# A hybrid decoder layer: weight sums on VectorE across the mLSTM, the last branch's weights stored split, and the branch projections' PSUM halves swapped

## The chip, the core and the metric

The kernel runs on one core of a Trainium2 chip. A core has a matrix engine (TensorE, PE in the profile), three engines for elementwise work (VectorE or DVE, ScalarE or ACT, GpSimd or POOL) and a queue engine (SyncE, SP) that issues most DMAs. Each engine works through its own instructions strictly in order and waits on semaphores for the others. The metric is the device time of one execution in microseconds (us).

## The reference

One layer of a decoder over 1024 positions of width 1024, in float32. After a normalisation, three branches run side by side on `h`: a chunkwise mLSTM, a differential attention, and a cross-attention into 256 memory tokens. Each branch's output is projected, multiplied by a sigmoid gate and summed; `w_out` and an MLP follow.

```python
h = rms_norm(x, norm_mix_g[l])
proj = h @ w_in[l]
...
y_m = jax.nn.sigmoid(mo) * rms_norm(hm, m_norm_g[l]...)          # mLSTM, chunks of 128 positions
y_d = diff_attention(dq, dk, dv, ...)
y_c = memory_cross_attention(cq, mem, ...)
g_m, g_d, g_c = jnp.split(jax.nn.sigmoid(h @ w_gate[l] + b_gate[l]), N_BRANCH, axis=-1)
merged = g_m * (y_m @ w_proj_m[l]) + g_d * (y_d @ w_proj_d[l]) + g_c * (y_c @ w_proj_c[l])
x = x + merged @ w_out[l]
h2 = rms_norm(x, norm_mlp_g[l])
x = x + jnp.square(jax.nn.relu(h2 @ w_up[l])) @ w_down[l]
```

## The kernel before

**Number format.** A matrix operand is kept as a pair: `hi`, the value rounded to the matrix engine's fast 32-bit format (`F32R`), and `lo`, what the rounding lost. A product is three matmuls: hi·hi, hi·lo, lo·hi. Making a pair is a *split*: ScalarE casts, VectorE subtracts (`split2`, `split`; their lines are L114 and L121 on ScalarE, L69 and L123 on VectorE).

**Stages.** Transposes and the memory branch (0 to about 196 us), the mLSTM (to 640), the differential attention (to 1150), the gates (`wino_gates`, to 1240), the three branch projections (`branches`, to 1478), `w_out` in four groups (to 1573), the MLP's up half (to about 1890) and its down half (to the end).

**The mLSTM.** TensorE's order is written out by hand: `weave(stream(), items)` walks along a stream of projection matmuls `mm<-hT,w` and calls the function of an item when its position in the stream comes. `add(p, f)` puts `f` at position `p`; the stream has about 520 positions. The items are the gate chain (`m_gates`, `m_gates2`: the tiles `g_two`, `g_m`, `g_c`, `g_col`), and eight half heads of four chunks. A chunk needs a mask tile `ngb`, a weight tile `wib` (both loaded from DRAM, where the gate chain stored them as `g_dng` and `g_dwi`), the running state `C` with its split `Ch`, and the output `hS` with its norm `hss`. Instructions outside TensorE's written order are placed by a scheduler, per engine.

**Branch projections.** Each of the three products of 1024x1024x1024 is computed by Winograd's scheme: 7 products of quadrants in place of 8, which needs sums of the quadrants of the weights `wq` and of the rows `y`. 84 steps: three branches in the order (2, 0, 1), seven passes each, four steps a pass, 12 matmuls of 128x512 a step. A step n also splits its weights (`w<-raw`) and its rows (`xs<-row`) five steps ahead. The result of a pass is in four PSUM banks; `evict` takes them through `te` tiles (or directly) to VectorE, which multiplies by the gates (`gl`, fetched from `gates`), adds the branches so far (`mg`) and splits the sum into `mh` and `ml`, the operands of `w_out`.

**The early sums.** For the sums that need only inputs, or results of the memory branch, `early_sums` runs ahead, during the mLSTM: 16 groups of four loads of 256 KB (tiles `es`, in the pool of the next stage's weights), four GpSimd additions or subtractions of 128x512 (L1443 to L1446, L1449 to L1452) and four stores (L1456) into DRAM (`ws`, `xc`). `branches` reads them back. They are added to the items at positions 20 to 486, but only TensorE's order is tied to these; the scheduler has put them between about 185 and 365 us.

**Banks and what follows.** The branch passes take PSUM banks in two halves (`mm0` to `mm3`, `mm4` to `mm7`) by turns; the four groups of `w_out` do too, and the MLP's first products follow in banks from `p0` on. The MLP's weights are Winograd sums too: `wino_steps` loads `wraw`, GpSimd makes four sums (L1292 to L1295) and ScalarE and VectorE split them into `wo`. The MLP's input norm needs `ssq`, a sum of squares that GpSimd builds during `w_out` (L1722), which TensorE adds up in `px<-ones,ssq`.

Of the kernel before, what the change touches and what calls it, by code (L numbers as in the profile page):

```python
# [10 lines left out]
F32 = mybir.dt.float32  # L11
F32R = mybir.dt.float32r
# [5 lines left out]
P = 128  # L18
D = 1024
S = 1024  # L20
# [11 lines left out]
def f32(ap):  # L32
    return ap.bitcast(F32)
# [40 lines left out]
class Layer:  # L74
# [11 lines left out]
    nmm, kmm = 0, 2  # L86
    turned, stored, relus = [], {}, {}
    marks = {}

    def pin(self, ins):  # L90
        if self.pinned:
            self.tc.keep_in_program_order(ins)

    def mm(self, out, l, r, start, stop):
        self.pin(self.nc.tensor.matmul(out, l, r, start=start, stop=stop))  # L95

    def transpose(self, out, x):
        self.pin(self.nc.tensor.transpose(out, x, self.ident))
# [360 lines left out]
    gnext = None  # L459
# [137 lines left out]
    def branch_m(self, pool, gp, tail, gnext):  # L597
        nc, a = self.nc, self.a
        V, G = nc.vector, nc.gpsimd
        W = 32  # L600
# [234 lines left out]
        one = lambda: next(piece, None)  # L835
# [35 lines left out]
        for n in range(8):  # L871
            hd, hf = heads[n // 2], n % 2
            e = Epos[n]
# [423 lines left out]
    def wino_steps(self, srcs, wrp, wop, lead):  # L1297


        raws, W = [], []  # L1300

        def raw():
            n = len(raws)
            if n < len(srcs):
                r = wrp.tile([P, 8, P], F32, tag="wraw", name=self.name("wraw"))
                self.nc.sync.dma_start(r[:, 0:4], srcs[n])
# [12 lines left out]
        return raw, wsp, W  # L1319
# [104 lines left out]
    PASS = ((0, 0), (1, 2), (4, 4), (3, 3), (5, 5), (6, 1), (2, 6))  # L1424
    WOUT = (0, 2, 4, 6, 1, 3, 5, 7)

    def early_sums(self, pool):

        G, a = self.nc.gpsimd, self.a
        dt = lambda n: self.nc.dram_tensor(n, (4, 4, P, 512), F32).ap()  # L1430
        self.ws = [dt(f"ws{b}") for b in range(3)]
        self.xc = dt("xc_d")

        def chunk(srcs, dst, rows):
            new = lambda: pool.tile([P, 2, 256], F32, tag="w", name=self.name("es")).rearrange("p a b -> p (a b)")
            t = [new() for _ in range(4)]
            for o, s in zip(t, srcs):
                self.nc.sync.dma_start(o, s)
            yield
            e = new()  # L1440
            b0, b1, b2, b3 = t
            if rows:
                G.tensor_sub(e, b2, b0)  # L1443
                G.tensor_sub(b0, b0, b1)
                G.tensor_sub(b2, b2, b0)
                G.tensor_sub(b3, b3, b2)  # L1446
                outs = (b0, b2, e, b3)
            else:
                G.tensor_sub(e, b1, b0)  # L1449
                G.tensor_add(b3, b3, b0)  # L1450
                G.tensor_sub(b0, b3, b1)
                G.tensor_sub(b2, b2, b0)  # L1452
                outs = (b3, b0, e, b2)
            yield
            for i, o in enumerate(outs):
                self.nc.sync.dma_start(dst[i], o)  # L1456
            yield

        for b in (2, 0, 1):
            for kp in range(4):  # L1460
                yield from chunk([a["wq"][b, i, kp] for i in range(4)], self.ws[b][:, kp], False)
        for kp in range(4):
            yield from chunk([self.y_quad(2, i, kp) for i in range(4)], self.xc[:, kp], True)

    def y_quad(self, b, i, kp):
        k, hf = divmod(i, 2)
# [2 lines left out]
    def branches(self, pools, fetch, hi, lo):  # L1469
# [13 lines left out]
        def load(n):  # L1483
            if n >= N + 4:
                return
            wr[n] = t = self.rp.tile([P, 512], F32, tag="raw", name=self.name("raw"))
# [12 lines left out]

        def split(n, f):  # L1500
            if n >= N + 4:
                return
            w = self.wp.tile([P, 2, 512], F32R, tag="w", name=self.name("w"))
            f(w[:, 0], w[:, 1], wr.pop(n))
            if n >= N:
                w0.extend((w[:, 0, i * 256 : i * 256 + 256], w[:, 1, i * 256 : i * 256 + 256]) for i in range(2))
# [3 lines left out]
            W[n], X[n] = w, x  # L1510
# [33 lines left out]
        def out(bi, u, m, hf, c, late):  # L1544
            ft = 2 * u + m
            t = gates.pop(0)
            if bi == 0:
                o = mg[ft, hf] = mlp.tile([P, 512], F32, tag="ml", name=self.name("mg"))
                V.scalar_tensor_tensor(out=o, in0=t, scalar=1.0, in1=c, op0=ALU.add, op1=ALU.mult)
            elif bi == 1:  # L1550
                V.scalar_tensor_tensor(out=t, in0=t, scalar=1.0, in1=c, op0=ALU.add, op1=ALU.mult)
                G.tensor_add(mg[ft, hf], mg[ft, hf], t)
            else:
                V.scalar_tensor_tensor(out=t, in0=t, scalar=1.0, in1=c, op0=ALU.add, op1=ALU.mult)
                (V if late else G).tensor_add(t, mg[ft, hf], t)

                def keep():
                    lo[ft, hf] = mlp.tile([P, 512], F32R, tag="ml", name=self.name("ml"))
                    hi[ft, hf] = mtp.tile([P, 512], F32R, tag="mh", name=self.name("mh"))
                    self.split2(hi[ft, hf], lo[ft, hf], t)  # L1560
                    gate()

                return keep
            gate()

        def evict(bi, p, u, ps):
            new = lambda i: te[i].tile([P, 512], F32, tag="te", name=self.name("te"))
            if p in (0, 3):
                T[u] = new(u)
                A.copy(T[u], ps)  # L1570
            elif p == 2:
                S[u] = new(4 + u)
                A.copy(S[u], ps)
            elif p in (1, 4):
                V.tensor_add(T[u], T[u], ps)
                return out(bi, u, *((0, 1) if p == 1 else (1, 0)), T[u], False)
            elif p == 5:
                V.tensor_add(S[u], S[u], ps)
                return out(bi, u, 0, 0, S[u], False)
            else:  # L1580
                return out(bi, u, 1, 1, ps, True)

# [80 lines left out]
    def tail(self):  # L1663
# [11 lines left out]
        with ExitStack() as c0:  # L1675
# [9 lines left out]
            with ExitStack() as c1:  # L1685
                E = lambda *x, **k: c1.enter_context(tc.tile_pool(*x, **k))
                self.pmm, self.kmm, self.nmm = Banks(E, "pmm2"), 8, 3
                if True:
# [5 lines left out]
                    te = [one(f"te{i}") for i in range(3)]  # L1694
                    hole = E(name="hole", bufs=1).tile([P, 256], F32, name="hole")
                    xd = E(name="xd", bufs=20)
                    te += [one(f"te{i}") for i in range(3, 8)]
# [478 lines left out]
```

## Time and profile before

| what | us |
|---|---|
| runs, median of 3 (lowest, highest) | 2207.85 (2203.75, 2211.08) |
| the profiled execution | 2204.02 |
| its span in the profile | 2202.2 |
| TensorE busy | 2126.5 |
| VectorE busy | 1560.5 |
| ScalarE busy | 1051.1 |
| GpSimd busy | 735.5 |

A line of the profile gives the source line and engine, the operation, its output and inputs by the program's names, and shapes. In a timeline the two first numbers are start and duration in us, and the brackets give the idle time of that engine just before, and what ended it. Matmuls of one kind in a row are one line, with their count behind an x. TensorE's clock is reported as the share of full speed that was granted. Many operations pass through helpers, so one line number (L69, L95, L114, L121, L123) stands for many places, and the tile names tell them apart.

### The profile page before, as it was taken

What the parts mean: (1) busy time and instruction counts of PE and PEld (TensorE: products, weight loads), DVE (VectorE), ACT (ScalarE), POOL (GpSimd) and SP (SyncE); (2) the same over time, 40 slices, a digit from 0 to 9 for tenths busy, and PEclk for the clock granted to TensorE, in tenths of its full rate; (3) what the DMA queues carried; (4) which work ended last, traced back from release to release, by engine and by line L of the source; (5) the groups of instructions that cost most, each with busy time, mean ns of one, the idle gap of its engine ahead of it and who ended that gap; (6) DMA issues with size and microseconds to landing.
All of it is one profiled execution on the core that took longest, in us unless ns stands there. A gap on an engine that the chain in (4) does not pass through costs nothing. (4 is left out here: it accounts for less than half of the span.)

```text
span 2202.2 us, 31307 instructions
## 1 busy us (share of the span) xinstructions
PE 2126.5 (97%) x10905; PEld 1836.4 (83%) x10905; DVE 1560.5 (71%) x2841; ACT 1051.1 (48%) x2155; POOL 735.5 (33%) x844
## 2 busy tenths in 40 slices
PE   7999798999999999999999999989899999999999
PEld 5888577898899999999887887778788888888887
DVE  6644565665557877777656588985378888876698
ACT  6643233544435666666545545354344544543331
POOL 2102553000011111111013044532445677665563
PEclk9999898999999999999999999999999999999999
DMA  6127675222144333333334784446524544844443
GB/s 241 40 72 247 233 243 182 68 64 71 42 169 104 97 96 87 88 93 87 106 126 133 260 299 141 137 135 221 174 84 156 208 157 157 298 158 155 158 158 106
DMA packets 167973, 322.16 MB, mean 146 GB/s; under 512 B 16737, under 2 KB 33414, under 8 KB 165766
## 3 DMA queue, kind: packets, MB, share of 16 engines
q1 hardware_dynamic: 161478, 300.22, 42.6%
q10 hardware_dynamic: 6336, 19.93, 2.3%
q8 instruction: 86, 1.41, 0.3%
q14 instruction: 73, 0.60, 0.1%
HBM read 206.81 MB, written 88.11 MB: 134 GB/s over the span
## 5 line engine op out<-in xcount | busy, mean ns | idle before, releaser
L95 PE MATMUL mm<-w,hT 128*128 128x384 f32 (+3 forms) x2496 | 473.4, 333 | 5.3 <-DVE gf L645 3.9
L95 PE MATMUL mm<-hT,w 128*128 128x512 f32 x1680 | 414.5, 398 | 0.9 <-ACT gt L500 0.9
L95 PEld LDWEIGHTS mm<-w,hT 128*128 128x128 f32 x2496 | 392.6, 191 | 16.3 <-issue 2.3
L95 PEld LDWEIGHTS mm<-hT,w 128*128 128x128 f32 x1680 | 313.1, 191 | 62.8 <-ACT gt L500 1.3
L95 PE MATMUL p<-xo,wo 128*128 128x512 f32 x1344 | 309.7, 392 | 6.5 <-DVE gl L1715 6.2
L95 PE MATMUL p<-xd,wo 128*128 128x512 f32 x1344 | 305.4, 389 | 0.4 <-DVE u L69 0.4
L95 PEld LDWEIGHTS p<-xo,wo 128*128 128x128 f32 x1344 | 253.7, 189 | 61.1 <-DVE gl L1715 7.3
L95 PEld LDWEIGHTS p<-xd,wo 128*128 128x128 f32 x1344 | 252.0, 188 | 53.6 <-DVE u L69 1.1
L1609 PE MATMUL mm<-xs,w 128*128 128x512 f32 x1008 | 232.4, 392 | 5.8 <-DVE xs L69 4.9
L1609 PEld LDWEIGHTS mm<-xs,w 128*128 128x128 f32 x1008 | 189.9, 189 | 48.2 <-DVE xs L69 7.4
L114 ACT CAST wo<-wraw 128x896 fp32r<-128x896 f32 x124 | 116.9, 945 | 225.8 <-PE p L95 85.4
L69 DVE TENSOR_TENSOR wo<-wraw,wo 128x896 fp32r<-128x896 f32 x124 | 151.1, 1228 | 47.2 <-ACT wo L114 47.1
L1292 POOL TENSOR_TENSOR wraw<-wraw 128x128 f32<-128x128 f32 x128 | 97.1, 758 | 220.4 <-DMA wraw<-in_wdown 109.1
L123 DVE TENSOR_TENSOR w<-raw,w 128x256 fp32r<-128x256 f32 (+4 forms) x257 | 141.3, 575 | 34.5 <-ACT w L121 33.9
L1041 ACT ACTIVATE dpe<-sc,dst,drr 128x256 f32<-128x256 f32 (+7 forms) x128 | 106.6, 833 | 97.2 <-DVE dst L1037 96.7
L121 ACT CAST w<-raw 128x256 fp32r<-128x256 f32 (+4 forms) x257 | 116.1, 487 | 49.8 <-PE mm L95 14.6
L148 POOL TENSOR_SCALAR drr<-drr 128x16 f32<-128x16 f32 x16 | 3.3, 204 | 311.0 <-DVE drr L988 311.0
L1033 DVE CUSTOM_DVE_ANT_0 sc<-sc,tmask 128x256 f32<-128x256 f32 (+7 forms) x128 | 97.0, 758 | 13.6 <-PE sc L95 12.8
L114 ACT CAST w<-raw 128x512 fp32r<-128x512 f32 x83 | 51.7, 624 | 90.2 <-DMA raw<-ws 45.6
L1294 POOL TENSOR_TENSOR wraw<-wraw 128x128 f32<-128x128 f32 x128 | 93.1, 727 | 0.0
L95 PE MATMUL sc<-dk,dq 128*128 128x512 f32 (+3 forms) x384 | 91.9, 347 | 0.0
L69 DVE TENSOR_TENSOR acc<-acc,p 128x512 f32<-128x512 f32 x121 | 79.9, 683 | 14.9 <-PE p L95 13.9
(338 smaller groups left out, 3524.5 us busy)
## 6 DMA issues: line engine op xcount, KB each, us to landing
dk<-dsg SPq DMA_DIRECT2D x64, 256.0 KB, 4.2
wraw<-in_wup SPq DMA_DIRECT2D x64, 256.0 KB, 3.1
r_d<-xts SPq DMA_DIRECT2D x16, 1024.0 KB, 4.7
wraw<-in_wdown SPq DMA_DIRECT2D x64, 256.0 KB, 3.1
es<-in_wq SPq DMA_DIRECT2D x48, 256.0 KB, 3.8
ws<-es SPq DMA_DIRECT2D x48, 256.0 KB, 2.0
raw<-in_wd SPq DMA_DIRECT2D x32, 384.0 KB, 3.3
raw<-ws SPq DMA_DIRECT2D x48, 256.0 KB, 3.4
```

The lines of the kernel that those rows point to most:

```text
L69: return self.tc.keep_in_program_order(f(*a, **k))
L95: self.pin(self.nc.tensor.matmul(out, l, r, start=start, stop=stop))
L114: self.cast = self.A.copy(hi, src).ins
L121: a = nc.scalar.copy(hi, src)
L123: return a, nc.vector.tensor_sub(lo, src, f32(hi))
L148: g.tensor_scalar(r, ss, 1.0 / width, EPS, op0=ALU.mult, op1=ALU.add)
L1033: V.tensor_tensor_reduce(out=sc[:, 0:n], in0=sc[:, 0:n], in1=self.tmask[:, D - n : D], scale=1.0, scalar=-3.0e38, op0=ALU.add, op1=ALU.max ...
L1041: nc.scalar.activation(pe[c][:, 0:n], sc[:, 0:n], AF.Exp, bias=t8[:, 2 + c : 3 + c], scale=rr[:, i, c : c + 1], accum_out=t8[:, 4 + c : 5 ...
L1292: G.tensor_add(r[:, 4], r[:, 0], r[:, 3])
L1294: G.tensor_sub(r[:, 6], r[:, 1], r[:, 0])
L1609: nc.tensor.matmul(cur[u], w[:, l, c], x[:, m], start=first and i == 0, stop=last and i == 2, skip_group_check=True)
```

## The change

1. `early_sums` becomes `early`. The 12 groups of sums for the branches 2 and 0 and the rows `xc` run on VectorE instead of GpSimd. For branch 1, the last, eight half groups (`pairs`) compute all seven weight combinations on VectorE and ScalarE, split them, and store the pairs hi|lo in DRAM (`wh`). Each step is tied to a stream position on every engine: `behind(ins, self.mark)` lets the scheduler place it only behind the matmul that stood last when the step was called. Loads stand at p, sums at p + 8, stores from p + 12. The groups start at 2, 19, 36 and then from 112 on, the last at 504.
2. In steps 56 to 83 (the last branch) `branches` loads the pair straight into the ring of split weights: no cast and no subtraction. Its addition at the sixth pass (p == 5) goes from GpSimd to VectorE.
3. The branch passes use the other half of the banks, with the four banks of a pass rotated by two; `nmm = 3` shifts the groups of `w_out` likewise, so that the last ends on the low half.
4. The first load of an MLP weight after this is tied behind the last branch matmul (`hold`). The `te` tiles stand in another order in memory.

```diff
-        early = self.early_sums(gnext)
-        for i in range(16):
-            for at in (20, 28, 36):
-                add(at + 30 * i, next, early)
+        self.early(gnext, add)
...
+    def early(self, pool, add):
...
+        self.wh = dt("wh", (7, 4, P, 2, 512))
...
+        def at(p, f):
+            def g():
+                for i in f():
+                    self.behind(i.ins, self.mark)
+
+            add(p, g)
...
+            return [(V.tensor_sub if o == "sub" else V.tensor_add)(*q) for o, *q in ops]
...
+            def cut(i):
+                q = t[i]
+                return [A.copy(q[:, 0], v(q)), V.tensor_sub(q[:, 1], v(q), f32(q[:, 0]))]
...
+            at(p, load)
+            at(p + 8, calc)
+            for i in range(7):
+                at(p + 10 + i, lambda i=i: cut(i))
+                at(p + 13 + i, lambda i=i: keep(i))
...
+        p = 2
+        for _ in range(3):
+            sums(p, *S.pop(0))
+            p += 17
+        p = 112
+        for n in range(8):
+            pairs(p, 1, n // 2, n % 2)
+            p += 29
+            sums(p, *S.pop(0))
+            p += 20
+        sums(p, *S.pop(0))
...
+            if 56 <= n < N:
+                bi, p, kp = where(n)
+                l, x = self.PASS[p]
+                W[n] = w = self.wp.tile([P, 2, 512], F32R, tag="w", name=self.name("w"))
+                nc.sync.dma_start(f32(w), self.wh[l, kp])
...
             elif p == 5:
                 V.tensor_add(S[u], S[u], ps)
-                return out(bi, u, 0, 0, S[u], False)
+                return out(bi, u, 0, 0, S[u], True)
...
-                        self.pmm.tile([P, 512], F32, tag=f"mm{4 - g % 2 * 4 + u}", name=self.name("mm")) for u in range(4)
+                        self.pmm.tile([P, 512], F32, tag=f"mm{g % 2 * 4 + (u + 2) % 4}", name=self.name("mm")) for u in range(4)
...
         self.pinned = False
+        self.hold = self.mark
...
-                    self.nmm = 7
+                    self.nmm = 3
```

SyncE's order where the gate chain's results go to DRAM and come back as the first `ngb` and `wib`, before:

```order
L1438 DMA es_3514<-in_wq 128x512
L581 DMA g_dng<-g_c 32x128
L582 DMA g_dwi<-g_u 32x128
L583 DMA g_dd<-g_mp 32x1
L1456 DMA ws<-es_3316 128x512
L718 DMA ngb_2514<-g_dng 128x4x128
L692 DMA wib_2508<-g_dwi 128x4x128
L585 DMA g_dec<-g_dd 128x32
```

and after:

```order
L585 DMA g_dwi<-g_u 32x128
L584 DMA g_dng<-g_c 32x128
L586 DMA g_dd<-g_mp 32x1
L695 DMA wib_2508<-g_dwi 128x4x128
L721 DMA ngb_2514<-g_dng 128x4x128
L588 DMA g_dec<-g_dd 128x32
```

The store of an early sum between the gate chain's stores and loads is gone, and the loads of `ngb` and `wib` have changed places.

VectorE's order at the third `ngb`, in the first half heads' chunks, before:

```order
L770 SCALAR_TENSOR_TENSOR C_3035<-C_2708,g_dec,sc_3025 128x258
L722 TENSOR_TENSOR ngb_3404<-ngb_3404,tmaskT 128x512
L123 TENSOR_TENSOR Ch_3037<-C_3035,Ch_3037 128x258
L778 TENSOR_TENSOR den_3040<-den_3040,g_col 128x1
L671 TENSOR_SCALAR cv_3053<-pre_3050,vec 128x512
L779 RECIPROCAL den_3040<-den_3040 128x1
```

and after:

```order
L773 SCALAR_TENSOR_TENSOR C_3062<-C_2719,g_dec,sc_3052 128x258
L725 TENSOR_TENSOR ngb_3454<-ngb_3454,tmaskT 128x512
L126 TENSOR_TENSOR Ch_3064<-C_3062,Ch_3064 128x258
L781 TENSOR_TENSOR den_3067<-den_3067,g_col 128x1
L1451 TENSOR_TENSOR es_3095<-es_2992,es_2991 128x256
L782 RECIPROCAL den_3067<-den_3067 128x1
L674 TENSOR_SCALAR cv_3080<-pre_3077,vec 128x512
L1451 TENSOR_TENSOR es_2991<-es_2991,es_2994 128x256
```

`ngb` still stands between `C` and `Ch`; the sums of `es`, four loads behind them, stand between the steps of the chunk and of the convolution `cv`.

VectorE's order at the end of the branches, the last pass but one and the operands of `w_out`, before:

```order
L69 TENSOR_TENSOR te_15371<-te_15371,mm_15357 128x512
L123 TENSOR_TENSOR wo_16501<-wraw_16495,wo_16501 128x7x128
L69 SCALAR_TENSOR_TENSOR gl_15611<-gl_15611,te_15371 128x512
L69 TENSOR_TENSOR te_15373<-te_15373,mm_15358 128x512
L69 SCALAR_TENSOR_TENSOR gl_15617<-gl_15617,te_15373 128x512
L69 TENSOR_TENSOR w_15666<-raw_15561,w_15666 128x512
L69 TENSOR_TENSOR ml_15681<-gl_15579,mh_15682 128x512
```

and after:

```order
L69 SCALAR_TENSOR_TENSOR gl_15750<-gl_15750,te_15540 128x512
L69 TENSOR_TENSOR gl_15750<-mg_14455,gl_15750 128x512
L69 TENSOR_TENSOR te_15542<-te_15542,mm_15527 128x512
L126 TENSOR_TENSOR wo_16637<-wraw_16631,wo_16637 128x7x128
L69 SCALAR_TENSOR_TENSOR gl_15756<-gl_15756,te_15542 128x512
L126 TENSOR_TENSOR w_16033<-raw_16031,w_16033 128x512
L69 TENSOR_TENSOR gl_15756<-mg_14460,gl_15756 128x512
L69 TENSOR_TENSOR w_15802<-raw_15703,w_15802 128x512
L69 TENSOR_TENSOR ml_15817<-gl_15721,mh_15818 128x512
```

The additions of `mg` now stand in VectorE's queue, the MLP weight's `wo` has moved back by three of the four tiles, and a split of `w_out`'s later weights stands between.

More of the change, by code (lines that the diff above doesn't have):

```diff
@@ L88 @@
     marks = {}
+    hold = None
     def pin(self, ins):
@@ L94, in mm @@
     def mm(self, out, l, r, start, stop):
-        self.pin(self.nc.tensor.matmul(out, l, r, start=start, stop=stop))
+        ins = self.nc.tensor.matmul(out, l, r, start=start, stop=stop)
+        self.mark = ins.ins
+        self.pin(ins)
     def transpose(self, out, x):
@@ L1305, in raw @@
                 r = wrp.tile([P, 8, P], F32, tag="wraw", name=self.name("wraw"))
-                self.nc.sync.dma_start(r[:, 0:4], srcs[n])
+                ins = self.nc.sync.dma_start(r[:, 0:4], srcs[n])
+                if self.hold:
+                    self.behind(ins.ins, self.hold)
+                    self.hold = None
                 self.wino_s(r)
@@ L1425 @@
     WOUT = (0, 2, 4, 6, 1, 3, 5, 7)
[L1427 to L1447, printed above, removed]
-            else:
[L1449 to L1463, printed above, removed]
@@ new lines, in early, with four, sums, load @@
+    def early(self, pool, add):
+        nc, V, A, a = self.nc, self.nc.vector, self.nc.scalar, self.a
+        dt = lambda n, s: nc.dram_tensor(n, s, F32).ap()
+        self.ws = {b: dt(f"ws{b}", (4, 4, P, 512)) for b in (2, 0)}
+        self.wh = dt("wh", (7, 4, P, 2, 512))
+        self.xc = dt("xc_d", (4, 4, P, 512))
+        def at(p, f):
[3 more added lines that the diff above has]
+            add(p, g)
+        def four(t, x):
+            r0, r1, r2, r3, e, f, g = t
+            if x:
+                ops = (("sub", e, r2, r0), ("sub", r0, r0, r1), ("sub", r2, r2, r0), ("sub", r3, r3, r2))
+            else:
+                ops = (("sub", e, r1, r0), ("add", r0, r0, r3), ("sub", f, r0, r1), ("sub", g, r2, f))
+            return [(V.tensor_sub if o == "sub" else V.tensor_add)(*q) for o, *q in ops]
+        new = lambda: pool.tile([P, 2, 256], F32R, tag="w", name=self.name("es"))
+        def sums(p, srcs, dst, x):
+            t = []
+            flat = lambda q: f32(q.rearrange("p a b -> p (a b)"))
+            def load():
+                t.extend(flat(new()) for _ in range(4))
+                return [nc.sync.dma_start(o, s) for o, s in zip(t, srcs)]
+            def calc():
+                t.extend([flat(new())] + ([None] * 2 if x else [t[1], t[2]]))
+                return four(t, x)
+            def store():
+                r0, r1, r2, r3, e, f, g = t
+                return [nc.sync.dma_start(dst[i], o) for i, o in enumerate((r0, r2, e, r3) if x else (r0, f, e, g))]
+            at(p, load)
+            at(p + 8, calc)
+            at(p + 12, store)
+        def pairs(p, b, kp, h):
+            t, s = [], slice(h * 256, h * 256 + 256)
+            v = lambda q: f32(q[:, 1])
+            def load():
+                t.extend(new() for _ in range(4))
+                return [nc.sync.dma_start(v(o), a["wq"][b, i, kp][:, s]) for i, o in enumerate(t)]
+            def calc():
+                t.extend(new() for _ in range(3))
+                return four([v(q) for q in t], False)
+            def cut(i):
+                q = t[i]
+                return [A.copy(q[:, 0], v(q)), V.tensor_sub(q[:, 1], v(q), f32(q[:, 0]))]
+            def keep(i):
+                l = (3, 0, 1, 2, 5, 4, 6)[i]
+                return [nc.sync.dma_start(self.wh[l, kp][:, :, s], f32(t[i]))]
+            at(p, load)
+            at(p + 8, calc)
+            for i in range(7):
+                at(p + 10 + i, lambda i=i: cut(i))
+                at(p + 13 + i, lambda i=i: keep(i))
+        S = [(([a["wq"][b, i, kp] for i in range(4)], self.ws[b][:, kp], False)) for b in (2, 0) for kp in range(4)]
+        S += [([self.y_quad(2, i, kp) for i in range(4)], self.xc[:, kp], True) for kp in range(4)]
+        p = 2
[9 more added lines that the diff above has]
+        sums(p, *S.pop(0))
@@ L1485, in load @@
                 return
+            if 56 <= n < N:
[3 more added lines that the diff above has]
+                nc.sync.dma_start(f32(w), self.wh[l, kp])
+                xr[n] = rows[bi, (1, 2, 3, 0, 1, 4, 3)[x], kp]
+                return
             wr[n] = t = self.rp.tile([P, 512], F32, tag="raw", name=self.name("raw"))
@@ L1502, in split @@
                 return
-            w = self.wp.tile([P, 2, 512], F32R, tag="w", name=self.name("w"))
-            f(w[:, 0], w[:, 1], wr.pop(n))
+            if not 56 <= n < N:
+                W[n] = w = self.wp.tile([P, 2, 512], F32R, tag="w", name=self.name("w"))
+                f(w[:, 0], w[:, 1], wr.pop(n))
             if n >= N:
+                W.pop(n)
                 w0.extend((w[:, 0, i * 256 : i * 256 + 256], w[:, 1, i * 256 : i * 256 + 256]) for i in range(2))
@@ L1509, in split @@
             f(x[:, 0], x[:, 1], xr.pop(n))
-            W[n], X[n] = w, x
+            X[n] = x
             bi, p, kp = where(n)
@@ L1693, in tail @@
                     one = lambda n, w=512: E(name=n, bufs=1, reuse_waits="tile")
-                    te = [one(f"te{i}") for i in range(3)]
+                    te = [one(f"te{i}") for i in range(4, 7)]
                     hole = E(name="hole", bufs=1).tile([P, 256], F32, name="hole")
                     xd = E(name="xd", bufs=20)
-                    te += [one(f"te{i}") for i in range(3, 8)]
+                    te = [one(f"te{i}") for i in range(4)] + te + [one("te7")]
                     gap = E(name="gap", bufs=1).tile([P, 512], F32, name="gap")
```

## The prediction

> **What bounds the kernel now.** I read the page first, then the waits of TensorE in stretches, then the rows around its two worst stretches.
>
> ```profile
> span 2202.2 us, 31307 instructions
> ...
> PE 2126.5 (97%) x10905; PEld 1836.4 (83%) x10905; DVE 1560.5 (71%) x2841; ACT 1051.1 (48%) x2155; POOL 735.5 (33%) x844
> ...
> PE   7999798999999999999999999989899999999999
> ...
> PEclk9999898999999999999999999999999999999999
> ```
>
> TensorE is busy for 2126.5 of 2202.2 us, so at most 75.7 us of idle time can be won, plus whatever its reduced clock costs. A slice is 55 us. Those that aren't 9 are the first, the 5th and 7th (220 to 385 us; the clock's digit falls to 8 there) and the 27th and 29th (1431 to 1596 us). The first group of the change works around the 5th to 7th, the rest in the last two. All sums below are made against the profiled execution, 2204.02 us (1.8 us of it outside the span), which lies 3.8 us under the median of the runs, 2207.85 us.
>
> The waits of TensorE from 150 to 420 us (line, what it waited for, us in total, times, longest):
>
> ```profile
> PE tp L95 <- DVE g_col L595: 9.9, 1, 9.9
> PE sc L95 <- DVE Ch L123: 6.1, 3, 5.4
> PE tp L98 <- DVE hS L791: 4.0, 3, 2.1
> PE mm L95 <- DVE gf L645: 3.9, 3, 2.1
> PE sc L95 <- ACT Ch L121: 2.3, 1, 2.3
> PE tp L555 <- DVE g_two L550: 2.0, 1, 2.0
> PE tp L564 <- DVE g_m L561: 2.0, 1, 2.0
> ```
>
> These come to 30.2 us, nearly all with VectorE's name. But VectorE is not the cause. The same stretch by windows (width, then busy us of PE, PEld, DVE, ACT, POOL; clock; DMA share; GB/s):
>
> ```profile
> 250.00:300.00 50.00, 39.87 (x186) 33.14 (x186) 17.80 (x33) 13.60 (x40) 24.07 (x19) 0.86 0.68 233
> 300.00:350.00 50.00, 38.97 (x166) 31.27 (x164) 35.07 (x52) 17.29 (x45) 25.84 (x21) 0.83 0.69 237
> 400.00:450.00 50.00, 50.00 (x335) 46.13 (x334) 35.40 (x91) 27.55 (x79) 3.85 (x4) 1.00 0.31 92
> 1400.00:1440.00 40.00, 35.83 (x147) 27.79 (x146) 35.78 (x41) 19.59 (x36) 22.40 (x14) 0.96 0.38 120
> ```
>
> Between 250 and 300 us VectorE works for 17.8 of 50 us while TensorE waits for it; between 400 and 450 us, in the same kind of work but with GpSimd nearly quiet, VectorE does 35.4 us and TensorE never stops. What VectorE waits for, and SyncE's queue at that moment:
>
> ```profile
> 266.00 0.69 DVE L722 TENSOR_TENSOR ngb<-ngb,tmaskT 128x512 f32<-128x512 f32 x1 [11.94 <-DMA ngb<-g_dng]
> ...
> 343.36 0.69 DVE L722 TENSOR_TENSOR ngb<-ngb,tmaskT 128x512 f32<-128x512 f32 x1 [9.02 <-DMA ngb<-g_dng]
> ...
> 425.59 0.69 DVE L722 TENSOR_TENSOR ngb<-ngb,tmaskT 128x512 f32<-128x512 f32 x1 [3.52 <-DMA ngb<-g_dng]
> ```
>
> ```profile
> 255.52 0.46 SPq L581 DMA_DIRECT2D g_dng<-g_c  x1
> ...
> 258.35 0.42 SPq L1456 DMA_DIRECT2D ws<-es  x1
> 262.16 0.39 SPq L718 DMA_DIRECT2D ngb<-g_dng  x1
> ```
>
> ```profile
> SPq L1456 <- POOL es L1449: 19.4, 7, 4.5
> ```
>
> VectorE's in-order queue stands at `ngb`, whose load stands in SyncE's in-order queue behind a store `ws<-es`, which waits for GpSimd's early sums (19.4 us behind L1449 alone, 185 to 400 us). At 425 us, with no such store near, the same load still costs VectorE 3.52 us, and TensorE doesn't notice.
>
> **1. The early sums leave GpSimd.** What they took there from 180 to 400 us (busy, mean ns, then idle before them and the releaser):
>
> ```profile
> L1450 POOL TENSOR_TENSOR es<-es,es 128x512 f32<-128x512 f32 x11 | 15.0, 1365 | 30.2 <-DMA es<-in_wq 30.2
> L1449 POOL TENSOR_TENSOR es<-es,es 128x512 f32<-128x512 f32 x11 | 14.7, 1335 | 40.5 <-DMA es<-in_wq 35.9 <-issue 4.7
> ```
>
> 64 such instructions go. What can come back is the idle time and the slow restart behind it:
>
> ```profile
> 280.14 2.94 PE L95 MATMUL mm<-hT,w 128*128 128x512 f32 x12
> ...
> 306.39 4.91 PE L95 MATMUL mm<-hT,w 128*128 128x512 f32 x12
> ```
>
> Twelve matmuls take 2.94 us when warm and 4.91 us at 306 us, behind three stalls of 2.11 us and less: 2.0 us lost. The windows bound all such loss: (1 − 0.86) × 50 + (1 − 0.83) × 50 = 15.5 us, of which idle time (21.2 us in these two windows) is a part; I take 10 us between 2 and 15.5. The Trainium skill ("TensorE: Matmul & The Clock Gate", Part 1: The HAM clock gate) has the clock halved only after an idle window of about 3.4 us. The row above disagrees, since its stalls are shorter; by the page's rule they would cost idle time alone, and the sum for these stalls would be about 2 us smaller.
>
> Of the 30.2 us I keep 12: about 4 at `g_col` (the pair of store and load of `g_dng` stays, at VectorE's normal wait of 3.52 us), 1 at the two `Ch`, 1 at `hS` (its `hss` stood behind an early sum on GpSimd), 2 at `gf`, 4 at the gate chain `g_two` and `g_m`, which has no early sum in it. So 18 us go, and 7 of the 10 us of slow restarts. Gain 25 us; bounds 0 (every wait has a second cause behind it) and 30 + 10 = 40.
>
> **2. The same sums on VectorE.** 48 sums of 128x512, 32 of 128x256, 56 casts on ScalarE and 56 subtractions of 128x256.
>
> ```profile
> L123 DVE TENSOR_TENSOR w<-raw,w 128x256 fp32r<-128x256 f32 (+4 forms) x257 | 141.3, 575 | 34.5 <-ACT w L121 33.9
> L121 ACT CAST w<-raw 128x256 fp32r<-128x256 f32 (+4 forms) x257 | 116.1, 487 | 49.8 <-PE mm L95 14.6
> 1406.89 0.68 DVE L69 TENSOR_TENSOR w<-raw,w 128x512 fp32r<-128x512 f32 x1
> ...
> 1409.19 1.77 DVE L69 TENSOR_TENSOR w<-raw,w 128x512 fp32r<-128x512 f32 x1
> ```
>
> At 0.68 us alone and 0.575 us as the mean of the half size: 48 × 0.68 + 88 × 0.575 = 83 us on VectorE, and 56 × 0.487 = 27 us on ScalarE, over the 440 us of the mLSTM. VectorE has 14.6 of 50 us free where it runs steadily (400 to 450 us), so 440 × 0.29 = 128 us; ScalarE has more. The throughput fits. The price is order. Each group's first operation waits for its four loads, and VectorE's next instruction stands behind it. The loads stand eight positions of the matmul stream ahead (520 positions in 440 us: about 7 us). Their landing in the page's list of DMA issues:
>
> ```profile
> es<-in_wq SPq DMA_DIRECT2D x48, 256.0 KB, 3.8
> ```
>
> That is 3.8 us, and four issues of about 0.4 us. The first three groups, in short steps, have about 3 us and may each wait 1 us or so. I take 2 us; bounds 0 and the slow rival below. Steady steps cover 3.5 us (the row at 425.59).
>
> Part 1 and 2 together: −23 us. The stores are spread too: 16 × 4 stores of 256 KB before; now 12 × 4 and 56, 27 MB against 17 MB. At 92 GB/s (400 to 450 us) against the 233 to 237 GB/s already seen, that hides.
>
> **3. Last branch: its weights come split.** 28 casts and 28 subtractions leave steps 56 to 83, and four adds move from GpSimd to VectorE (4 × 0.68 = 2.7 us). The waits of TensorE from 1400 to 1490 us, and three rows:
>
> ```profile
> PE mm L95 <- DVE ml L69: 5.3, 1, 5.3
> PE mm L1609 <- DVE xs L69: 3.3, 4, 2.1
> ```
>
> ```profile
> 1436.15 4.37 PE L1609 MATMUL mm<-xs,w 128*128 128x512 f32 x11 [2.15 <-DVE xs L69]
> ...
> 1476.92 1.19 DVE L123 TENSOR_TENSOR wo<-wraw,wo 128x896 fp32r<-128x896 f32 x1 [2.11 <-ACT wo L121]
> ```
>
> Here VectorE does bind: 35.78 of 40 us busy. A step is 12 matmuls, some 2.9 us, and each loses a subtraction of 0.68 to 1.77 us. The 3.3 us of waits for `xs` go, with a slow restart of 4.37 − 11 × 0.245 = 1.7 us at 1436: 5 us. The 5.3 us before `w_out` go only in part: `wo` still stands ahead of the last `gl` and `ml`, its load now issues behind the last gates' loads, and VectorE, with three of the adds ahead of it, reaches it at about the same time. I keep 2.6 and give back 2.7, bounds −2 and 7 (the slow restart with it). Part 3: −8 us; bounds −3 (the `wo` load later by 2 us) and −12. The 28 loads are twice as large, 28 × 256 KB = 7.3 MB more over 76 us: 96 GB/s on top of the 120 of the window from 1400 us, well under the 237 already seen.
>
> **4. Bank halves.** At the start, the third and fourth tile of the first pass now fall on banks that the last evictions of the stage before still read:
>
> ```profile
> 1240.35 2.88 PE L1609 MATMUL mm<-xs,w 128*128 128x512 f32 x12
> ...
> 1242.42 0.68 DVE L1261 TENSOR_TENSOR u<-u,mm 128x512 f32<-128x512 f32 x1
> ```
>
> At 2.88 / 4 = 0.72 us a tile TensorE wants the third at 1241.8 and the fourth at 1242.5, and the eviction ends at 1243.1: +1 us, bounds 0 and 1.5. At the end, the MLP's first run no longer waits for `w_out`'s last group:
>
> ```profile
> 1582.79 6.69 PE L95 MATMUL p<-xo,wo 128*128 128x512 f32 x21 [3.14 <-DVE gl L1715]
> 1589.31 1.84 PE L95 MATMUL px<-ones,ssq 128*128 128x1 f32 x16
> ...
> 1586.04 3.34 POOL L1722 TENSOR_TENSOR ssq<-ssq,sq 128x512 f32<-128x512 f32 x1
> ```
>
> This wait and part of one like it six us before go, but `px<-ones,ssq`, a little further in TensorE's order, starts at 1589.3 us, when the last `ssq` sum ends (1589.4 us), and that chain doesn't change. TensorE arrives earlier and waits there: −1 us, bounds −3 and +2 (a longer single wait with its restart).
>
> **Sum.** −25 + 2 − 8 + 1 − 1 = −31 us: 2173 us for the profiled execution, and 2177 us from the median; I say 2174.
>
> **Rivals.** (a) **VectorE blocks at the early sums' loads, and it comes out slower.** On GpSimd, L1449 and L1450 waited 35.9 + 30.2 = 66.1 us for loads in 12 groups, 5.5 us each. If the 20 groups on VectorE wait so, each beyond the 3.5 us of cover, TensorE loses 2.0 us and a restart of 2.0 us: 20 × 4 = 80 us, 2204 − 31 + 80 = 2253 us. It beats the whole gain (31 + 6.6 us) at 1.9 us per group. Against it: those loads were issued by a SyncE queue stuck behind the very stores, and now each operation is placed eight positions behind its load. (b) **The mLSTM's waits have a second cause** (the gate chain, the round trip of `g_dng`; or part of (a) eats the gain): only parts 3 and 4 remain, −8 us, 2196 us, 2200 from the median. For it: 3.5 us of `ngb` remain in each chunk. Against: 400 to 450 us runs with that wait and no stall. (c) **All of it comes back**: −40 − 12 and nothing new, 2152 us. (d) **The change doesn't relieve the end of the branches** (the `wo` chain and the larger loads take it): −23, 2181 us, within my forecast's surroundings.
>
> **How the numbers follow.** Forecast 0.58, (a) 0.06, (b) 0.16, (c) 0.14, (d) 0.06. A measurement of this kernel tells about 0.3% (6.6 us) from no change. Forecast, (c) and (d) are faster; (b) lies on that bound, so I halve it: faster 0.86, same 0.08, slower 0.06. The range reaches from (c) to (b)'s far side: 2150 to 2200; what is left out is (a), a part of (b) and more than full recovery.
>
> **What would show it.** Part 1: the waits from 150 to 420 us fall from 30 to about 12 us, the clocks of 0.86 and 0.83 rise above 0.95, and `ngb` waits 3 to 5 us each time. Part 2: VectorE waits for DMAs of `es` under 1 us a group; TensorE shows none. Part 3: no wait for `xs` from 1400 us on, one of 2 to 3 us for `ml`. Part 4: one wait of 6 to 9 us at `px` in place of that of 3.14 us and its like. I'd be wrong above all if VectorE's waits for `es` pass 3.5 us, or if a new wait follows `ngb` behind the stores to `wh`.

## The result and the profile after

| | runs, median (lowest to highest), us | profiled execution, us | span, us |
|---|---|---|---|
| before | 2206.59 (2203.75 to 2211.08) | 2204.02 | 2202.2 |
| after | 2179.43 (2178.04 to 2184.54) | 2178.04 | 2176.2 |

The kernel before has one run more here than in the table further up, hence another median. The ratio is 0.9879, with a 95% interval of 0.9856 to 0.9903: 27 us faster, by 1.2%. The forecast was 2174 us in a range of 2150 to 2200.

The page of the changed kernel, the rows shown of before:

```profile
span 2176.2 us, 31507 instructions
...
PE 2117.4 (97%) x10905; PEld 1829.7 (84%) x10905; DVE 1556.2 (72%) x2953; ACT 1055.3 (48%) x2183; POOL 642.2 (30%) x776
...
PE   7999999999999999999999999999899999999999
...
PEclk9999999999999999999999999999899999999999
```

The gap at 220 to 385 us is closed. One at 1523 to 1577 us (the 29th slice, now of 54 us) has stayed, in the clock too. The waits of TensorE from 150 to 420 us, 32.5 us before (30.2 in the seven rows shown further up), are down to 9.5, of which these are the larger:

```profile
PE tp L101 <- DVE hS L794: 2.6, 2, 1.3
PE mm L96 <- DVE gf L648: 2.0, 3, 1.2
PE sc L96 <- ACT Ch L124: 1.9, 2, 1.5
PE tp L101 <- DVE tho L801: 1.1, 1, 1.1
PE sc L96 <- DVE Ch L126: 1.0, 3, 0.4
```

And the windows of the same stretch (columns as before: PE busy, PEld, DVE, ACT, POOL; clock; DMA share; GB/s):

```profile
250.00:300.00 50.00, 50.00 (x257) 42.19 (x256) 32.28 (x79) 26.44 (x72) 1.20 (x2) 1.00 0.49 160
300.00:350.00 50.00, 46.55 (x280) 40.94 (x279) 36.15 (x94) 25.68 (x75) 1.47 (x2) 1.00 0.64 206
450.00:500.00 50.00, 44.37 (x266) 39.70 (x264) 38.85 (x97) 25.40 (x74) 4.53 (x4) 0.97 0.72 230
```

The clock is 1.00 where it was 0.86 and 0.83. But idle time has spread to the later mLSTM (TensorE worked for all 50 us from 450 to 500 before), and three new waits stand in the profile: for the load `w<-wh`, at the start of the branches, and at `px`. The starts of the stages in the timelines of TensorE say what each stretch became:

| stretch of TensorE (us) | before | after | difference |
|---|---|---|---|
| start to the first branch matmul | 1240.35 | 1216.53 | −23.8 |
| branches, to the first `mm<-mh,w` | 238.09 | 239.51 | +1.4 |
| from there to the last `px<-ones,ssq` | 110.87 | 106.10 | −4.8 |
| from there to the end of the span | 612.89 | 614.06 | +1.2 |

### The profile page after: what moved, and what is told of

Read it like the earlier page. It is cut to its first block, busy times and chain, and to the rows that moved or that the text cites. A ratio compares the mean times of both kernels' runs of the same rounds, so it can differ in the third digit from the quotient of the medians.

```text
span 2176.2 us, 31507 instructions
## 1 busy us (share of the span) xinstructions
PE 2117.4 (97%) x10905; PEld 1829.7 (84%) x10905; DVE 1556.2 (72%) x2953; ACT 1055.3 (48%) x2183; POOL 642.2 (30%) x776
## 4 chain that ended last, share of the span: by engine, by line
PE 77%; DVE 9%; DMA 7%; ACT 2%; issue 2%; POOL 1%; SPq 0%; DVEq 0%; ACTq 0%; POOLq 0%
PE mm L96 30%; PE p L96 28%; PE mm L1668 7%; PE sc L96 5%; PE po L96 3%; PE tp L101 3%; DMA xr<-h_d 1%; DMA es<-in_wq 1%; DVE w L126 1%; DVE xs L69 1%; DVE cv L678 1%; DVE w L69 1%; DVE es L1451 1%; DMA raw<-in_wd 1%; PE pr L101 1%
## 5 line engine op out<-in xcount | busy, mean ns | idle before, releaser
L96 PE MATMUL mm<-hT,w 128*128 128x512 f32 x1680 | 408.2, 393 | 0.3 <-ACT gt L503 0.3
L96 PEld LDWEIGHTS mm<-hT,w 128*128 128x128 f32 x1680 | 308.2, 188 | 60.7 <-ACT gt L503 0.9
L126 DVE TENSOR_TENSOR w<-raw,w 128x256 fp32r<-128x256 f32 (+4 forms) x257 | 127.6, 521 | 28.1 <-ACT w L124 27.5
L151 POOL TENSOR_SCALAR hss<-hss 128x4 f32<-128x4 f32 x8 | 6.1, 765 | 429.7 <-ACT mscr L785 429.7
```

The costliest lines, as they stand in the source:

```text
L96: ins = self.nc.tensor.matmul(out, l, r, start=start, stop=stop)
L126: return a, nc.vector.tensor_sub(lo, src, f32(hi))
```

## The experiments

Twelve kernels ran, each with the kernel before on the same chip. Ratios are to that kernel before. A hundredth of a ratio is 22 us. Comparisons between two experiments go by ratios, since the kernel before had medians of 2204 to 2208 us in these sets of runs. Stages are read from one profiled execution of each kernel; where two kernels have the same code in a stage, it still differs by 1 us or so (the branches take 238.09 us in before, 239.31 in e5 and 237.99 in e6).

| kernel | us, median | ratio (95% interval) |
|---|---|---|
| after | 2179.43 | 0.9879 (0.9856 to 0.9903) |
| e1: after, no split ahead | 2177.42 | 0.9875 (0.9859 to 0.9890) |
| e2: after, sums on GpSimd | 2196.60 | 0.9959 (0.9948 to 0.9971) |
| e3: after, groups not tied | 2173.58 | 0.9862 (0.9847 to 0.9877) |
| e4: after, old bank halves | 2171.91 | 0.9850 (0.9835 to 0.9864) |
| e5: before, sums on VectorE | 2174.81 | 0.9871 (0.9856 to 0.9885) |
| e6: before, sums tied, on GpSimd | 2174.63 | 0.9868 (0.9854 to 0.9883) |
| e7: after, loads from wh in turn | 2172.26 | 0.9865 (0.9848 to 0.9882) |
| e8: e7, old banks, not tied | 2164.92 | 0.9825 (0.9810 to 0.9839) |
| e9: e7, old banks | 2169.31 | 0.9835 (0.9818 to 0.9851) |
| e10: e1, old banks | 2172.60 | 0.9845 (0.9830 to 0.9860) |
| e11: after, no hold | 2178.78 | 0.9872 (0.9856 to 0.9886) |
| e12: before, new bank halves | 2209.30 | 1.0020 (1.0010 to 1.0031) |

### Which part pulls: e1 to e4

**e1**, nothing split ahead (four more groups of sums stand in for the eight half groups):

```diff
-            pairs(p, 1, n // 2, n % 2)
+            if n % 2:
+                sums(p, *S.pop(0))
...
-            if 56 <= n < N:
+            if False:
```

> The changed kernel, but the last branch's weights are not split ahead: its four groups of sums run on VectorE at every other place of the eight half groups, and the casts and subtractions are back in steps 56 to 83. Theory 'the split ahead pays for itself': the waits for xs (3.3 us before the change, and a restart of 1.7) and that for ml come back by 5 to 9 us against the 4.7 us wait for the load from wh that goes: 2180 to 2184 us. Rival 'the new wait eats all of it': 2174 to 2179 us. In both the mLSTM's end stays within 2 us of the changed kernel's.

**e2**, all sums of the early groups on GpSimd, at the same places:

```diff
-            return [(V.tensor_sub if o == "sub" else V.tensor_add)(*q) for o, *q in ops]
+            return [(G.tensor_sub if o == "sub" else G.tensor_add)(*q) for o, *q in ops]
```

> The changed kernel, with all sums of the early groups on GpSimd again, still tied to their places in the stream. Theory 'places': what was won in the mLSTM came from tying loads, sums and stores to places, so that SyncE's queue no longer stands behind stores: 2178 to 2186 us, TensorE's waits from 150 to 640 us under 25 us. Rival 'engine': GpSimd's slow sums and what they do to VectorE were the cost: 2194 us or more, and the waits on ngb of 9 to 12 us are back.

**e3**, on VectorE, but not tied to places:

```diff
-                for i in f():
-                    self.behind(i.ins, self.mark)
+                f()
```

> The changed kernel, with the early groups on VectorE but no longer tied: the scheduler places them as it likes. Theory 'places': they gather again early in the mLSTM, SyncE's queue stands behind their stores and VectorE behind their loads: 2192 to 2215 us. Rival 'engine': VectorE does them in half the time wherever they stand, 2178 to 2185 us.

**e4**, the old bank halves:

```diff
-tag=f"mm{g % 2 * 4 + (u + 2) % 4}"
+tag=f"mm{4 - g % 2 * 4 + u}"
...
-                    self.nmm = 3
+                    self.nmm = 7
```

> The changed kernel with the bank halves as before (4 - g%2*4 + u, and the last group of w_out on the high half). Theory 'the wait only moves': the start of the branches gains 1.6 us, the waits for gl before the MLP (6 us) stand in place of those at px: 2177 to 2182 us. Rival 'the halves are worth the 6 us': 2184 to 2187 us.

e1 came out at 2177 us, in the range of the rival, and its ratio can't be told from the changed kernel's. But its mLSTM missed the expectation. Its first branch matmul starts at 1208.20 us, 8.3 us ahead of the changed kernel, with waits of TensorE from 190 to 640 us of 11.4 us against 17.1. So the split ahead costs the mLSTM 8 us. What it brings later is in the rest of e1's timeline: branches of 237.07 us (2.4 less than after) and 110.99 us (4.9 more) to `px`. As made, the split ahead is worth nothing that the runs could show.

e2 and e3 spoke for the engine and against the places: on GpSimd at places 2196.6 us, on VectorE without places 2173.6, better than either range that I had given for it. The `ngb` waits of 9 to 12 us, though, that I expected of e2 did not come back. SyncE's queue in e2, from 190 to 640 us, and what its first line waits for:

```profile
SPq L1470 <- POOL es L1452: 52.3, 30, 5.5
```

Thirty waits behind GpSimd's sums, but none longer than 5.5 us. With eight half groups, e2 asks GpSimd for 80 sums in place of 64 and VectorE for the splits besides, so it is no fair test of places. What costs it 18.5 us against the changed kernel ahead of the branches (1235.07 against 1216.53 us) isn't shown. Two things differ in the traces: VectorE waits 8.6 us there for GpSimd's sums, to split them, and its own operations run longer, as the next section shows.

e4 was a plain miss: 0.9850 against 0.9879, some 6 us better than the changed kernel, with intervals that overlap a little. It speaks for a cost of the swapped halves; e12 tests that alone.

### One thing at a time on the kernel before: e5, e6

**e5**:

```diff
-        G, a = self.nc.gpsimd, self.a
+        G, a = self.nc.vector, self.a
```

> The kernel before, with one word changed: the 64 early sums run on VectorE; nothing is tied, nothing is split ahead, the banks are as before. Theory 'engine' (the early groups had to leave GpSimd, wherever they stand): most of the 24 us won ahead of the branches, so 2180 to 2190 us. Rival 'places': 2197 us or more.

**e6**, on GpSimd, each load, sum and store tied as the change ties them:

```diff
-            for at in (20, 28, 36):
-                add(at + 30 * i, next, early)
+            for at in (2, 10, 14):
+                add(at + 32 * i, next, early)
...
+        tie = lambda i: self.behind(i.ins, self.mark)
...
-                self.nc.sync.dma_start(o, s)
+                tie(self.nc.sync.dma_start(o, s))
...
-                G.tensor_sub(e, b1, b0)
+                tie(G.tensor_sub(e, b1, b0))
```

> The kernel before, with the early sums on GpSimd but loads, sums and stores tied to places: groups at 2 + 32 i, sums 8 behind the loads, stores 4 behind the sums. Theory 'engine': 2196 us or more, within 10 us of before. Rival 'places' (SyncE's queue behind the stores was all): 2180 to 2190 us.

Both came out alike, 0.9871 and 0.9868, better than their ranges, and neither can be told from the whole change (0.9879). So neither "engine" nor "places" falls; on the kernel before, either is enough. VectorE's waits for `ngb` from 180 to 420 us, in before, e5 and e6 (us in total, times, longest):

```profile
DVE ngb L722 <- DMA ngb<-g_dng: 29.6, 4, 11.9
```

```profile
DVE ngb L722 <- DMA ngb<-g_dng: 10.0, 3, 4.6
```

```profile
DVE ngb L724 <- DMA ngb<-g_dng: 21.1, 5, 5.2
```

The total doesn't decide, but where a wait stands and how long it is. In before, the waits of 11.94 and 9.02 us are followed by stalls of TensorE of 9.87 us (at `g_col`) and 5.44 us (at `Ch`). In e6 two early ones of 4.88 and 2.76 us are still followed by stalls of 3.12 us (at `mpT`) and 2.16 us (at `Ch`), the later ones, up to 5.21 us, by none above 0.2 us.

The two long waits of before have different causes, and the reading in the prediction holds for one of them. At 343 us it is the queue. The load of `ngb` needs the tile that VectorE's `mpT` frees at 333.00 us, but it is issued at 339.25 us, behind stores that wait for GpSimd's sums:

```profile
336.13 3.03 SPq L1456 DMA_DIRECT2D xc_d<-es  x3
339.25 0.39 SPq L718 DMA_DIRECT2D ngb<-g_dng  x1
```

In e6 the same load is issued at 345.42 us, right behind its `mpT`, which ends at 345.39 us. At 266 us, the longer wait, it is not the queue. What SyncE waits for there is the landing of the gate chain's own store of `g_dng`, which the load reads:

```profile
SPq L718 <- DMA g_dng<-g_c: 3.3, 1, 3.3
```

That store of 16 KB took 6.6 us from issue to landing; in e5, e6 and the changed kernel it took 1.7, 1.4 and 1.4 us. The store `ws<-es` at 258.35 us waited 1.4 us for GpSimd, but it was issued before that landing, so it cost this load nothing. Ten transfers of 256 KB had been issued in the 8 us ahead of `g_dng`; whether these held it up isn't shown (e5 issued seven in the 6.4 us ahead of its own).

There is a third cost of sums on GpSimd, which the prediction leaves out: VectorE's own operations run longer beside them. The same 112 splits from 180 to 640 us, before and after (count, then busy us and mean ns):

```profile
L123 DVE TENSOR_TENSOR w<-raw,w 128x256 fp32r<-128x256 f32 x112 | 56.5, 532 | 8.7 <-ACT w L121 8.7
L126 DVE TENSOR_TENSOR w<-raw,w 128x256 fp32r<-128x256 f32 x112 | 43.9, 418 | 3.0 <-ACT w L124 3.0
```

Their mean is 418 ns in e5 too, 468 in e6 and 508 in e2. The last steps of the gate chain (L567, L572, L577) take 1.1 to 1.3 us each in before, and 0.2 to 0.3 us in e2, e5, e6 and the changed kernel. So e5 and e6 win the same 29 us by two ways, and in neither do slow sums come many at once. Which of the three costs has which share of the 29 us isn't separated by any run.

The windows from 300 to 350 us of e5 and e6:

```profile
300.00:350.00 50.00, 46.20 (x275) 40.64 (x274) 40.87 (x97) 26.48 (x77) 1.52 (x2) 0.97 0.74 241
```

```profile
300.00:350.00 50.00, 46.81 (x284) 41.39 (x284) 31.12 (x77) 25.79 (x74) 12.25 (x10) 1.00 0.57 184
```

DMA traffic is as high in e5 as it was before (241 against 237 GB/s), and TensorE does 46.2 us of work in place of 39.0. So the amount of traffic in that window wasn't the cause.

### The load of the split weights: e7

The changed kernel's SyncE queue in the last branch, and TensorE:

```profile
1383.58 0.39 SPq L1540 DMA_DIRECT2D w<-wh  x1
1386.56 0.32 SPq L1731 DMA_DIRECT2D gl<-gates  x1
1386.98 0.38 SPq L1540 DMA_DIRECT2D w<-wh  x1
```

```profile
1391.78 64.43 PE L1668 MATMUL mm<-xs,w 128*128 128x512 f32 x276 [4.72 <-DMA w<-wh]
```

The load that TensorE needs at 1387.06 us is issued at 1386.98 us and lands 4.8 us later. SyncE's order there (numbers rise with the steps):

```
L1540 DMA w_15251<-wh 128x1024
L1731 DMA gl_15241<-gates 128x512
L1731 DMA gl_15245<-gates 128x512
L1540 DMA w_15299<-wh 128x1024
L1731 DMA gl_15271<-gates 128x512
L1540 DMA w_15189<-wh 128x1024
```

`w_15189`, the sixth load (step 61), stands behind those of steps 64 and 66, and behind three fetches of gates that wait for a free `gl`. The ring of eight slots is taken at the split for steps up to 55 (5 ahead) and at the load from 56 on (9 ahead), so the order around step 56 is 52, 56, 53, 57, 54, 58, 55, 59, 60, 61: step 61 gets the slot of step 56, not 53. The slots of 53, 54 and 55 go to steps 62, 64 and 66 and come free sooner, so their loads stand ahead.

```diff
             if 56 <= n < N:
-                W[n] = w = self.wp.tile([P, 2, 512], F32R, tag="w", name=self.name("w"))
-                nc.sync.dma_start(f32(w), self.wh[l, kp])
...
             if not 56 <= n < N:
...
+            else:
+                W[n] = w = self.wp.tile([P, 2, 512], F32R, tag="w", name=self.name("w"))
+                nc.sync.dma_start(f32(w), self.wh[self.PASS[where(n)[1]][0], where(n)[2]])
```

> The changed kernel, with each load from wh issued, and its slot taken, where the split of that step stood (5 steps ahead) in place of 9 steps ahead, so that the ring of eight slots is taken in the order of the steps. Theory 'slot and queue' (the load of step 61 got the slot of step 56 and then stood in SyncE's queue behind a fetch of a gate): the wait of 4.7 us at w<-wh falls under 1 us, 2173 to 2176 us. Rival 'bandwidth' (the loads of 512 KB land in 8 us there whatever their order): a wait of 3 us or more stays, 2177 to 2184 us.

The wait is gone altogether; from 1333 us on TensorE runs without a stop in the branches:

```profile
1333.46 117.05 PE L1669 MATMUL mm<-xs,w 128*128 128x512 f32 x515 [1.70 <-DVE xs L69]
```

The branches take 233.04 us in place of 239.51. A load of 512 KB with a shorter lead does better, since it isn't out of turn. The wait for `w<-wh` is in every kernel that loads 9 steps ahead (4.7 us after, 3.7 in e3, 3.8 in e4, 4.0 in e11) and in none that loads in turn (e7, e8, e9). The slowest of e7's loads still takes 9.2 us to land, so the rival "bandwidth" falls. By ratios the whole is 0.0014 better (3 us), with intervals that overlap; e9 against e4 says the same (0.0015). Why the whole shows 3 us where the stage shows 6.5 isn't known.

### The sums of parts: e8 to e11

**e8** joins e7's edit, e4's and e3's. **e9** is e8 with the ties:

> The changed kernel, with the old bank halves, the early groups not tied, and the loads from wh in turn. If the three effects add (7, 0 to 5, and 3 to 4 us): 2163 to 2169 us. If the gains overlap: 2170 to 2174 us, no better than the old banks alone.

> e8 with the early groups tied to their places again: the changed kernel with the old bank halves and the loads from wh in turn. If ties cost nothing on VectorE: 2163 to 2167 us, as e8. If the late groups are what stalls TensorE at 420 to 640 us (hS, 4.4 us): 2167 to 2171 us.

e8 is the best of all, 0.9825, and beats both kernels. e9 lies 2 us behind it by ratios, with intervals that overlap. A wait of about 4 us for `hS` in the later mLSTM is in the kernels with tied sums on VectorE (4.4 after, 4.2 in e9, 3.6 in e10, which has no split ahead), and not in e3 and e8, where they aren't tied (1.6 at most). In the changed kernel it reads, on TensorE and on VectorE just before:

```profile
500.66 1.26 PE L101 MATMUL tp<-ident,hS 128*128 128x128 f32 x4 [4.40 <-DVE hS L794]
```

```profile
496.79 0.69 DVE L1451 TENSOR_TENSOR es<-es,es 128x512 f32<-128x512 f32 x1 [1.73 <-DMA es<-y]
497.40 0.69 DVE L126 TENSOR_TENSOR kh<-cv,kh 128x512 fp32r<-128x512 f32 x1
498.00 0.68 DVE L1451 TENSOR_TENSOR es<-es,es 128x512 f32<-128x512 f32 x1
```

VectorE stands for an early sum's load and then does four sums, while `hS`, whose norm `hss` GpSimd finished at 493.19 us, waits its turn. That is my rival (a), at one place out of twenty. But the length of such waits alone doesn't price them: in e3 VectorE waits up to 4.9 us for `es`, and TensorE's waits for `hS` there come to 1.6 us.

**e10** (e1 with e4's edit):

> e1 with the old bank halves: no split ahead, sums on VectorE at places. Theory 'the split ahead costs about 8 us in the mLSTM and wins 4 to 5 in the branches and 5 at w_out, once its loads come in turn': 2168 to 2173 us, 3 us or more over e9. Rival 'it isn't worth its stores': 2166 us or less. The effect of the banks, by e4, should be 5 to 7 us against e1's 2177.

0.9845, against e9's 0.9835: the split ahead, with its loads in turn, wins 2 us, less than the 3 that I gave it; the intervals overlap. By stages of the two profiles, e10's mLSTM ends 7.4 us sooner, its branches take 6.4 us more and the stretch up to `px` 6.5 us more. Against e4 (0.9850), where the loads are out of turn, it is even.

**e11**:

```diff
-        self.hold = self.mark
+        self.hold = None
```

> The changed kernel without the tie of the first MLP weight behind the last branch matmul. VectorE's order is the same, so 2177 to 2182 us, no difference. Rival: the load comes earlier and holds GpSimd and VectorE in the last branch, 2183 us or more with a wait for ml of 3 us.

No difference, as expected: the hold decides nothing here.

### The bank halves on the kernel before: e12

It is e4's edit the other way round, made on the kernel before.

> The kernel before with the bank halves of the change alone (rotated tags, the last group of w_out on the low half). Theory 'the swap costs 6 to 7 us wherever it is made' (as e4 against the change, e9 against e7, e10 against e1): 0.2 to 0.4% slower than before, 2210 to 2214 us, with a wait at the branches' start and one of about 5 us at px. Rival 'it only collides with what else the change did' (my forecast for it was no change): within 0.1% of before.

1.0020, from 1.0010 to 1.0031: the swap alone makes the kernel slower. With e4 against after (0.0029), e9 against e7 (0.0030) and e10 against e1 (0.0030), its price is 4 to 7 us in four settings; the intervals within those three pairs overlap a little, and e12's alone is clear of 1. What it consists of is plainest in e12. Its branch stage is 1.9 us longer, by the wait at its start:

```profile
1243.22 7.11 PE L1609 MATMUL mm<-xs,w 128*128 128x512 f32 x30 [1.87 <-DVE hole L1699]
```

The releaser that it names, `hole`, is a write of 0.06 us that stands right behind the eviction `u<-u,mm` of 1242.48 us in VectorE's order; with the old halves it stands there too, and nothing waits.

And before the MLP, first e12, then e4 (old halves):

```profile
1584.97 1.02 PE L95 MATMUL px<-ones,ssq 128*128 128x1 f32 x8 [2.45 <-DVE gl L1715]
1591.50 1.87 PE L95 MATMUL px<-ones,ssq 128*128 128x1 f32 x8 [5.51 <-POOL ssq L1722]
1593.23 17.41 PE L95 MATMUL p<-xo,wo 128*128 128x512 f32 x66
```

```profile
1550.20 6.68 PE L96 MATMUL p<-xo,wo 128*128 128x512 f32 x21 [4.36 <-DVE gl L1775]
1556.72 1.84 PE L96 MATMUL px<-ones,ssq 128*128 128x1 f32 x16
1558.42 15.27 PE L96 MATMUL p<-xo,wo 128*128 128x512 f32 x66
```

The `ssq` chain decides when `px` runs, in both. With the old halves TensorE waits for a bank first, restarts slowly (21 matmuls in 6.68 us, 0.32 each) and reaches `px` just as `ssq` is done: the slow restart lies within the chain. With the new halves it does those matmuls at once, waits at `px` itself (2.45 us for a bank, then 5.51 us for `ssq`), and restarts slowly behind it: 66 matmuls take 17.41 us against 15.27, 2.1 us, with nothing to cover them. They take 16.6 to 17.8 us in all seven kernels with the new halves, and 15.25 to 15.27 us in all seven with the old. From `px` to the end of the span the new halves cost 2.1 to 3.0 us in each of the four pairs; the stages ahead of `px` differ by −1.4 to +6.0 us, without a pattern.

The chain itself holds another queue: GpSimd waits 4.2 us for the load of an MLP weight, does its four sums, and only then the last sum of `ssq` (e4 and e12). No run tried it in another order.

## Why the prediction came out as it did

**What bounds the kernel**: right that GpSimd's bunched sums were behind the gap; e5 and e6 relieve them by two ways, and both close it. But the path that the prediction gave, SyncE's queue behind a store, is shown for the wait at 343 us only. The longer one, at 266 us, was the landing of the store of `g_dng` (6.6 us against 1.4), and the longer operations of VectorE beside GpSimd were left out.

**Part 1 and 2, −23 us**: measured −23.8 to the first branch matmul. The waits of TensorE from 190 to 640 us fell from 32.5 to 17.1 us (the sum of the view's rows). In all, TensorE's idle time ahead of the branches fell by 16.7 us and its busy time, for the same matmuls, by 7.2 us (1187.3 to 1180.1), which I put down to the restarts, since the clock of the windows rose with it. My terms were 18 and 7. But part 2 was too small: I gave 2 us to VectorE's waits for the loads and held the throughput for covered. Without the split ahead the mLSTM ends 8.3 us sooner (e1), so 23.8 is some 32 less 8. The throughput itself was no trouble: the 136 new operations took 68.0 us, not 83 (0.575 us was the mean of a group with other shapes in it; those of 128x256 took 0.42), and VectorE's busy time ahead of the branches rose by only 20.3 us, because its other operations got shorter. VectorE's waits for `es` were 7.7 us in 7 places, the longest 2.8 us, at the loads from `in_wq`, and one of 1.7 us at those from `y`; they are not the 5.5 us a group of rival (a), since the loads stood ahead of the sums, as argued. They are above the 1 us that I named as the sign, though, and TensorE does show one of them, at 500 us.

**Part 3, −8 us**: the branches grew by 1.4 us, of which 1.6 is the wait at their start (part 4), so −0.2 there. The waits for `xs` from 1400 us on went, as forecast. The term that failed is the one that hid the loads: I weighed them by GB/s (96 on top of 120) and not by the slot and the queue in which each waits. That gave 4.7 us of wait, and with its restart (29 matmuls in 8.44 us, 0.29 each, against 0.23) most of the 6.5 us that e7 takes off the branches. The wait for `ml` fell to 0.8 us, where I kept 2.6:

```profile
1457.27 0.50 PE L96 MATMUL mm<-ml,w 128*128 128x512 f32 x1 [0.84 <-DVE ml L69]
```

VectorE reaches `wo` at 1453.13 us and doesn't wait for it; the stretch up to `px` got its 4.8 us mainly from that.

**Part 4, 0 us**: wrong, though each half of the mechanism was there. The wait at the start was 1.56 us (I said 1). The wait at the end did move to `px`, 2.42 and 4.95 us there, where I said one of 6 to 9. I counted it at −1, because TensorE arrives earlier; behind `px` alone it cost 2.1 to 3.0 us, because the chain sets the end and the restart now lies behind it. The sum of part 4 is about +6 us (e4, e9, e10), 4 to 5 on the kernel before (e12), beyond the +3.5 of my bounds.

**The sum**: 2177 us from the median by the working, 2174 as given, 2179 measured. That it came so near is luck, since errors of both signs met: the relief was 5 us and more larger than I gave (e5 and e6: 28 to 29 us), the splitting in the mLSTM and the banks cost 6 us each more.

The Trainium skill ("TensorE: Matmul & The Clock Gate", Part 1: The HAM clock gate) asks for an idle window of about 3.4 us before the clock is halved. The wait of 5.51 us at `px` in e12, with a granted clock of 0.50 in the 3.8 us behind it, agrees. The stalls of 2.11 us and less at 303 to 306 us before do not (0.58 in the 4.9 us behind them), nor does the single one of 2.15 us at 1436 us (0.61 in the 4.35 us behind it).

What stays open: why untied groups (e3, e8) do 2 to 4 us better than tied ones isn't settled beyond the `hS` wait, and the intervals overlap. How the swap's +4 to +7 divides between the start and `px` was read from profiles, not tried apart. How the 29 us divide between the queue, the late landing and the longer operations is open, as is what makes e2 so slow. The addition that went to VectorE and the new order of the `te` tiles were not tried alone.

## What to carry to other kernels

When an engine idles for another that idles too, follow the chain to the in-order queue that both stand behind; here, at one of two places, stores waiting for a slow engine held the load of something else. Check at each place what the queue waits for: at the other it was a small store that landed late. Either a faster producer or a spread in time was enough. A prefetch can be late by its slot and its place in the issuing queue, as here by 4.7 us, where bandwidth would have been enough: check in which order a ring's slots are taken when the lead changes on the way. And where a slow chain sets the next step, a wait inside its time is free with its restart, and a wait at its end isn't, since the restart behind the last wait is paid in full.

## What the runs showed of the hardware

Ahead of the branches, 16.7 us less idle time of TensorE came with 7.2 us less busy time for the same matmuls: the slow restarts cost there somewhat under half of what the stalls cost. After the wait at `px` the next 66 matmuls lost 1.3 to 2.5 us in the seven kernels that have it, and after the wait of 4.72 us for `w<-wh` the branches lost about 1.8 us beside it (6.5 − 4.7). A stall of 2.15 us was followed by a granted clock of 0.61 for 4.35 us (1436 us, before), one of 1.67 us by a clock of 1.00 (1354 us, before).

The same VectorE split of 128x256 took 532 ns on average with GpSimd's sums bunched beside it, and 418 ns without them. A store of 16 KB landed 6.6 us after its issue in before, where ten transfers of 256 KB had been issued in the 8 us ahead of it, and 1.4 us after it in the changed kernel.
